# Modulation of a hybrid diffusion backbone: from split weights and vector-engine sums to unsplit float32 matmuls in 32-column tiles

## The chip, the cores and the metric

The kernel runs on one core of one Trainium2 chip. The metric is the device time of one execution in microseconds, as a median over several runs. The engines are PE (matmuls; its weight loads are listed apart as PEld), DVE (vector), ACT (scalar activations), POOL (GpSimd) and SP, which here only issues transfers. Each engine runs its own instructions in a fixed order; semaphores hold an instruction back until what it reads is there.

## The reference, cut to what matters

One layer over 256 latent and 256 context tokens of width 1024. A condition vector `c` (and `c_ctx` for the context) gives six rows of 1024 numbers through `w_ada`, a matrix of 1024 x 6144:

```python
mod = silu(cond) @ w_ada + b_ada
sh1, sc1, g1, sh2, sc2, g2 = split(mod, 6)
pl = split_cols((rms_norm(x) * (1 + sc1) + sh1) @ w_in)     # the context likewise, with c_ctx
x  = x + g1 * (concat(mlstm(pl, pc), hgrn2(pl, pc)) @ w_out)
h  = rms_norm(x) * (1 + sc2) + sh2
x  = x + g2 * moe(h)                                        # top 4 of 32 experts
return rms_norm(x) * final_g
```

`sh1` and `sc1` are wanted at the start, for the latent and for the context; `g1`, `sc2`, `sh2` after the two mixers, and `g2` by the experts, for the latent alone. The mixers are two-directional scans (mLSTM and HGRN2, four heads each), preceded by 3x3 depthwise convolutions. Everything is float32. The 32 experts read 400 MB of weights.

## The kernel before

Tokens stand in 512 columns: 0 to 255 are context, 256 to 511 latent. All large weights come by `load_rows` (L115): a transfer of 1 MB on SP's queue into the next of five buffers of 128 x 2048 (`ring`; for the experts eight and two more). A load can be issued when the buffer five loads earlier has been read out. A projection reads its weight in two halves: `halves` (L86 to L88) makes `wh`, the rounded part (ACT, L87), and `wl`, the rest (DVE, L88), 1024 columns at a time into a pool of three, and three fp32r products, `hh` x `wh`, `hl` x `wh` and `hh` x `wl`, take the place of one in float32 (`proj_cols`, L273 to L275; `proj_tok`, L290 to L292).

A scheduler lays out each engine's order when the kernel is built, from the dependencies, the order of writing and priorities; on the chip the order is fixed, and an instruction that waits holds up all that stand behind it on its engine.

The modulation is done in three ways. Columns 0 to 2047 (`sh1`, `sc1`) go through `halves` like any weight, sixteen of them: the condition (two columns and their rounding rests, `silr`) is the stationary side with 4 columns, and 64 products 4x512 (L239, L240) sum into four banks; `arow`, sixteen small products with `fold4` (L248), `mod` and `gain` follow. The other columns are summed on DVE: `gemv(i, ...)` (L586) runs over eight slices of 128 x 1024 and adds each, times its entry of the condition, to `aacc`; then `row` (L625) sums over the partitions and spreads the row by two float32 products with a matrix of ones, and ACT copies it out (L626). Rows 2 and 4 are summed in `hgrn_inputs(0)`, row 3 after `hgrn_scan(0)`, row 5 (`g2`) late, with its products after the output projection `project(1)`. The sixteen gate columns of `w_in` (`wg`, a transfer of 64-byte pieces) are split into `wgh`, `wgl` (L226, L227) and multiplied in 24 products (L352 to L354).

After the modulation the written order is: projections and scan of the first HGRN2 head pair (`hgrn_inputs(0)`, `hgrn_scan(0)`), of the second pair, the mLSTM inputs and scan (L695 to L741), the output gates (`out_gate`, by `proj_tok`), the output projection, norm and router, and then the experts (L900 to L990). In a scan, L481 is the product on the diagonal, L502 the product of a doubling step, L505 the masked copy behind it, and L531 and L532 update `WW` for the next step.

Of the kernel before, what the change touches and what calls it, by code (L numbers as in the profile page):

```python
# [9 lines left out]
FT = mybir.dt.float32  # L10
FR = mybir.dt.float32r
# [4 lines left out]
OP = mybir.AluOpType  # L16
# [12 lines left out]
def tile_hybrid_backbone(  # L29
# [96 lines left out]
    aacc = [fo.tile([128, D], FT, name=f"aacc{i}") for i in range(3)]  # L126
# [60 lines left out]
    dve.tensor_mul(silc, silc, ptr[:, 0:16])  # L187
    silr = fc.tile([128, 8, 4], FR, name="silr")
    silv = silc.rearrange("p (w k) -> p k w", w=2)
    dve.tensor_copy(silr[:, :, 0:2], silv)  # L190
    dve.tensor_sub(silr[:, :, 2:4], silv, silr[:, :, 0:2].bitcast(FT))
    fold4 = fc.tile([4, 2], FT, name="fold4")
    dve.tensor_add(fold4, ident[0:4, 0:2], ident[0:4, 2:4])
# [25 lines left out]
    wgh = px.tile([128, 8, 128], FR, name="wgh")  # L219
    wgl = px.tile([128, 8, 128], FR, name="wgl")  # L220
    nc.gpsimd.memset(wgh.bitcast(FT), 0.0)
    nc.gpsimd.memset(wgl.bitcast(FT), 0.0)
    wg4 = wg.rearrange("p a (g h) -> p a g h", g=4)
    wgh4 = wgh.rearrange("p a (g r) -> p a g r", g=4)[:, :, :, 0:4]
    wgl4 = wgl.rearrange("p a (g r) -> p a g r", g=4)[:, :, :, 0:4]
    dve.tensor_copy(wgh4, wg4)  # L226
    dve.tensor_sub(wgl4, wg4, wgh4.bitcast(FT))  # L227


    pa = [pj.tile([128, 512], FT, name="pj") for _ in range(4)]  # L230
    for g in range(2):
        for q in range(4):
            w = wa.pop(0) if wa else load_rows(w_ada[0], 256 * q, 2, g * D, D)
            for i in range(2):
                k = 2 * q + i
                wh, wl = halves(w[:, i])
                for n in range(2):
                    s = slice(n * 512, (n + 1) * 512)
                    mm(pa[2 * g + n][0:4, :], silr[:, k], wh[:, s], start=(k == 0), stop=False)  # L239
                    mm(pa[2 * g + n][0:4, :], silr[:, k], wl[:, s], start=False, stop=(k == 7))  # L240

    arow = px.tile([4, 2048], FT, name="arow")
    for n in range(4):
        (act(arow[:, n * 512:(n + 1) * 512], pa[n][0:4, :], AF.Copy) if n % 2 else
         dve.tensor_copy(arow[:, n * 512:(n + 1) * 512], pa[n][0:4, :]))
    pt = bank()
    for b in range(16):
        mm(pt[:, 2 * b:2 * b + 2], arow[:, b * 128:(b + 1) * 128], fold4, start=True, stop=True)  # L248
    mod = fc.tile([128, 16, 2], FT, name="mod")
    dve.tensor_tensor(mod, pt[:, 0:32].rearrange("p (b w) -> p b w", w=2),  # L250
                      cols[:, col["ba"]:col["ba"] + 16].unsqueeze(2).to_broadcast([128, 16, 2]), op=OP.add)
# [179 lines left out]
    def hgrn_inputs(hp, parts=None):  # L431
# [27 lines left out]
    def hgrn_scan(hp, fgt, hq, hv):  # L459
# [114 lines left out]
        return last  # L574

    def gemv(i, dst, after, qs=range(4)):

        if qs[0] == 0:
            nc.gpsimd.memset(dst, 0.0)
            nc.gpsimd.dma_start(dst[0:1, :], b_ada[0:1, i * D:(i + 1) * D])  # L580
        for q in qs:
# [37 lines left out]
    g1b, sc2, sh2 = aacc[0:3]

    def row(i, dst):
        for n in range(2):
            f = slice(n * 512, (n + 1) * 512)
            p_ = bank(True)
            mm(p_, ones, aacc[i][:, f], start=True, stop=True)  # L625
            act(dst[:, f], p_, AF.Identity, bias=one_c) if i == 1 else act(dst[:, f], p_, AF.Copy)  # L626
# [13 lines left out]
    aacc.append(ep.tile([128, D], FT, name="aacc3"))  # L640
# [3 lines left out]
    dve.tensor_mul(sc2, sc2, n2b)  # L644
# [3 lines left out]
    for k in range(8):  # L648
        nc.gpsimd.dma_start(shc[:, k:k + 1], sh2[0:1, k * 128:(k + 1) * 128])
# [185 lines left out]
    gemv(5, aacc[3], scan_end)  # L835
# [23 lines left out]
    nc.gpsimd.dma_start(x2, x[0].rearrange("(a p) d -> p a d", p=128))  # L859
    nc.gpsimd.dma_start(bgs, b_gu[0].rearrange("e (b f) -> (e b) f", f=128).rearrange("(g p) f -> p g f", p=128))  # L860
# [9 lines left out]
    with tc.issue_after(last_e[0].ins):  # L870
        row(3, g2b)
# [237 lines left out]
```

## Time and profile before

| what | value |
|---|---|
| median of 3 runs | 1292.71 us (1290.19 to 1296.00) |
| profiled execution, its own time | 1289.07 us |
| its span | 1287.1 us |
| mean granted TensorE clock | 0.986 of full |
| PE, DVE, ACT, POOL busy | 1165.2, 479.4, 267.9, 110.8 us |
| bytes moved | 455.77 MB |

The span is the time from the first to the last instruction of the profiled execution; some 2 us lie outside it. Busy shares are means over stages with different limits, so the table by stretch (below) says more than they do. Matmuls are pipelined: a product's duration in a row is longer than its distance to the next, and where a price is wanted the distance between starts is the one to take.

### The profile page before, as it was taken

The page shows a single profiled execution, that of the slowest core. Times are in us where ns is not written, and L with a number is a line of the kernel's source. Part 1 is how long each engine was busy: PE and PEld are TensorE (multiplying, and loading weights), DVE is VectorE, ACT ScalarE, POOL GpSimd, SP SyncE. Part 2 cuts the span into 40 slices and gives each one's busy share as a digit, 9 for nine tenths or more (in the row PEclk, how much of TensorE's full clock was granted, in tenths as well). Part 3 has the DMA queues.
Part 4 walks back from the last instruction along what each step waited for, and adds up shares of the span by engine and source line. Part 5 has one row for each costly group of instructions (what it writes and reads, how often), then busy time and mean ns, then how long its engine had stood idle before and what let it go on. Part 6 is the DMA issues. An engine that isn't in the chain of part 4 may idle for free.

```text
span 1287.1 us, 14502 instructions
## 1 busy us (share of the span) xinstructions
PE 1165.2 (91%) x5706; PEld 557.3 (43%) x5709; DVE 479.4 (37%) x983; ACT 267.9 (21%) x492; POOL 110.8 (9%) x199
## 2 busy tenths in 40 slices
PE   4899999998999998889999998998899889889994
PEld 1578998896534342333323422422243234223221
DVE  7889999687112221312112221121211121112124
ACT  5666566563100000001000100100010001000001
POOL 5000000301111010101101100110020002000001
PEclk8899999999999999999999999999999999999998
DMA  9583533349699999999999999999999999999994
GB/s 331 199 294 129 180 102 128 116 173 411 271 416 418 415 418 416 405 417 416 416 416 416 417 417 417 417 417 417 416 417 417 418 417 415 417 417 417 417 415 178
DMA packets 99738, 455.77 MB, mean 354 GB/s; under 512 B 8809, under 2 KB 25282, under 8 KB 66896
## 3 DMA queue, kind: packets, MB, share of 16 engines
q1 hardware_dynamic: 97104, 452.62, 87.7%
q0 software_dynamic: 1200, 1.56, 0.4%
q8 instruction: 47, 0.77, 0.2%
q10 hardware_dynamic: 1360, 0.60, 0.2%
q14 instruction: 27, 0.22, 0.0%
HBM read 453.69 MB, written 1.05 MB: 353 GB/s over the span
## 4 chain that ended last, share of the span: by engine, by line
PE 55%; DMA 37%; DVE 4%; ACT 2%; issue 1%; ACTq 0%; DVEq 0%; SPq 0%
PE pu L940 19%; DMA w<-w_gu_dram 19%; DMA w<-w_down_dram 17%; PE pd L973 9%; PE pm L922 5%; PE pm L985 3%; PE pj L275 2%; PE pj L273 2%; PE pj L274 2%; DVE wl L88 1%; PE pj L292 1%; PE pt L949 1%; DMA wg<-w_in_dram 1%; PE pj L290 1%; PE pj L291 1%
## 5 line engine op out<-in xcount | busy, mean ns | idle before, releaser
L940 PE MATMUL pu<-w,XT 128*64 128x512 f32 x2048 | 470.3, 599 | 31.9 <-DMA w<-w_gu_dram 31.9
L940 PEld LDWEIGHTS pu<-w,XT 128*64 128x64 f32 x2048 | 135.6, 136 | 324.1 <-issue 223.5
L973 PE MATMUL pd<-w,aT 128*64 128x512 f32 x1024 | 240.8, 601 | 16.5 <-DMA w<-w_down_dram 14.9
L956 DVE TENSOR_TENSOR gl<-pt,bgT 128x512 f32<-128x512 f32 x32 | 22.1, 692 | 319.0 <-PE pt L949 318.9
L76 ACT ACTIVATE gu<-pu 128x512 f32<-128x512 f32 x48 | 26.9, 595 | 504.8 <-PE pu L940 504.8
L973 PEld LDWEIGHTS pd<-w,aT 128*64 128x64 f32 x1024 | 65.1, 136 | 152.1 <-issue 101.4
L78 DVE COPY gu<-pu 128x512 f32<-128x512 f32 x16 | 11.1, 692 | 276.4 <-ACT gu L76 276.4
L976 DVE TENSOR_TENSOR YP<-pd,g2b 64x512 f32<-64x512 f32 x64 | 44.1, 689 | 116.8 <-PE pd L973 116.2
L922 PEld LDWEIGHTS pm<-S,h 128*128 128x128 f32 x512 | 65.5, 199 | 47.7 <-issue 44.4
L913 POOL TENSOR_SCALAR S<-islot,posm 128x64 f32<-128x64 f32 x60 | 25.5, 446 | 690.4 <-PE pm L928 660.0
L922 PE MATMUL pm<-S,h 128*128 128x128 f32 x512 | 75.8, 294 | 1.2 <-DVE S L913 1.0
L985 PE MATMUL pm<-YP,GT 128*128 128x512 f32 x128 | 62.6, 615 | 11.0 <-DVE YP L976 11.0
L88 DVE TENSOR_TENSOR wl<-w,wh 128x1024 fp32r<-128x1024 f32 x55 | 66.7, 1221 | 6.5 <-ACT wh L87 6.3
L87 ACT ACTIVATE wh<-w 128x1024 fp32r<-128x1024 f32 x55 | 57.6, 1062 | 44.9 <-PE pj L274 21.8
L924 ACT ACTIVATE XT<-pm 128x512 f32<-128x512 f32 x32 | 19.1, 597 | 224.4 <-PE pm L922 224.4
L275 PE MATMUL pj<-hh,wl 128*128 128x512 f32 (+1 forms) x160 | 58.1, 368 | 3.0 <-DVE wl L88 3.0
L274 PE MATMUL pj<-hl,wh 128*128 128x512 f32 (+1 forms) x160 | 59.0, 370 | 0.0
L273 PE MATMUL pj<-hh,wh 128*128 128x512 f32 (+1 forms) x160 | 58.6, 372 | 0.0
L949 PE MATMUL pt<-ident,gu 128*128 128x128 f32 x256 | 38.8, 282 | 15.2 <-ACT gu L76 15.2
L949 PEld LDWEIGHTS pt<-ident,gu 128*128 128x128 f32 x256 | 27.3, 141 | 53.1 <-ACT gu L76 32.8
L959 ACT ACTIVATE sg<-gl 128x512 f32<-128x512 f32 x32 | 20.2, 630 | 128.5 <-DVE gl L957 128.5
L916 POOL TENSOR_SCALAR G<-islot,posm,gate 128x64 f32<-128x64 f32 x64 | 44.4, 709 | 5.5 <-DVE cnt_i L893 5.0
(455 smaller groups left out, 1210.1 us busy)
## 6 DMA issues: line engine op xcount, KB each, us to landing
w<-w_gu_dram SPq DMA_DIRECT2D x256, 1024.0 KB, 19.9
w<-w_down_dram SPq DMA_DIRECT2D x128, 1024.0 KB, 20.1
w<-w_ada_dram SPq DMA_DIRECT2D x24, 1024.0 KB, 6.4
w<-w_in_dram SPq DMA_DIRECT2D x16, 1024.0 KB, 6.0
w<-w_out_dram SPq DMA_DIRECT2D x4, 1024.0 KB, 5.0
xin<-x_dram SPq DMA_DIRECT2D x1, 1024.0 KB, 7.3
xin<-ctx_dram SPq DMA_DIRECT2D x1, 1024.0 KB, 12.2
x<-x_dram POOLq DMA_DIRECT2D x1, 1024.0 KB, 5.4
```

Of the source, the lines that this page charges most:

```text
L87: act(wh, src, AF.Copy)
L88: dve.tensor_sub(wl, src, wh.bitcast(FT))
L273: mm(o, wh[:, s], hh[:, k, t0:], start=(k == 0), stop=False)
L274: mm(o, wh[:, s], hl[:, k, t0:], start=False, stop=False)
L275: mm(o, wl[:, s], hh[:, k, t0:], start=False, stop=(k == 7))
L916: nc.gpsimd.tensor_scalar(G[:, a, j], islot, pos_of(a, j), gate_of(a, j), op0=OP.is_equal, op1=OP.mult)
L922: mm(p_[:, i * ns:(i + 1) * ns], h2[:, a, (k + i) * 128:(k + i + 1) * 128], S[:, a, 0:nj].rearrange("p j s -> p (j s)"), start=(a == 0), s ...
L940: mm(ps[64 * j:64 * j + 64, n * 512:(n + 1) * 512], XT(k), w[:, 0, j * 1024 + n * 512:j * 1024 + (n + 1) * 512], start=(k == 0), stop=(k = ...
L949: nc.tensor.transpose(pt[:, f * 128:(f + 1) * 128], s[:, f * 128:(f + 1) * 128], ident)
L973: mm(pd_[64 * n:64 * n + 64, :], aT[:, k], w[:, i, n * 512:(n + 1) * 512], start=(k == 0), stop=(k == 7))
L976: dve.tensor_mul(yp[:, f], pd_[64 * n:64 * n + 64, :], g2b[64 * n:64 * n + 64, f])
L985: mm(p_, GTs[j][0:ns, a * 128:(a + 1) * 128], YP[0:ns, j, n * 512:(n + 1) * 512], start=(j == 0), stop=(j == np_ - 1))
```

## The change

The six rows now come from three calls of `gemv(gp)`, 2048 columns each. A call loads eight slices of 128 rows x 2048 columns (one contiguous piece of 8 KB on each partition, where before it was two of 4 KB). For each slice four unsplit float32 products, 128 x 32 on 128 x 512, go to four blocks of 32 partitions of one bank; the 32 stationary columns hold the two conditions and 30 zeros. Call 0 feeds `mod` and `gain` through one copy and four transposes. Calls 1 and 2 are in `rows`, written behind `hgrn_inputs(0)` and behind `hgrn_inputs(1)`: DVE adds the bias, POOL sends the row to DRAM and reads it back spread over the partitions; `g2b` is read back later. `shc`, once eight small transfers, comes from four transposes. The sums on DVE, the products with ones and sixteen of the splits are gone. The modulated tokens are now written in place in `hT`; the gate columns are unsplit too, in eight float32 products with 32 columns, and one product with `sel4` adds their four blocks.

```diff
-    wa = [load_rows(w_ada[0], 0, 2, 0, D)]
     nc.sync.dma_start(xin[:, 2:4], x[0].rearrange("(a p) d -> p a d", p=128))
-    wa.append(load_rows(w_ada[0], 256, 2, 0, D))
     nc.sync.dma_start(xin[:, 0:2], cx[0].rearrange("(a p) d -> p a d", p=128))
...
-    dve.tensor_copy(wgh4, wg4)
-    dve.tensor_sub(wgl4, wg4, wgh4.bitcast(FT))
...
+    dve.tensor_copy(wgp[:, :, 0:16], wg)
...
+    def gemv(gp):
+
+        pa = pj.tile([128, 512], FT, name="pj")
+        for k in range(8):
+            w = load_rows(w_ada[0], 128 * k, 1, 2 * D * gp, 2 * D)
+            for j in range(4):
+                mm(pa[32 * j:32 * j + 32, :], silr[:, k], w[:, 0, j * 512:(j + 1) * 512], start=(k == 0), stop=(k == 7))
+        return pa
+
+    def columns(p_, row):
+
+        for i in range(4):
+            nc.tensor.transpose(p_[:, i * 128:(i + 1) * 128], row[:, i * 128:(i + 1) * 128], ident)
+        return p_.rearrange("p (c j r) -> p j c r", c=4, j=4)
+
+    pa = gemv(0)
+    arow = px.tile([128, 512], FT, name="arow")
+    act(arow, pa, AF.Copy)
...
+        hm = hT[:, k]
+        act(hm[:, 0:256], hm[:, 0:256], AF.Identity, bias=mod[:, k, 1:2], scale=gain[:, k, 1:2])
+        dve.tensor_scalar(hm[:, 256:], hm[:, 256:], gain[:, k, 0:1], mod[:, k, 0:1], op0=OP.mult, op1=OP.add)
         act(hh[:, k], hm, AF.Copy)
...
+    pg4 = pj.tile([128, 512], FT, name="pj")
+    for k in range(8):
+        mm(pg4[32 * (k % 4):32 * (k % 4) + 32, :], wgp[:, k], hT[:, k], start=(k < 4), stop=(k >= 4))
+    gq = px.tile([128, 512], FT, name="gq")
+    act(gq, pg4, AF.Copy)
     pg = pj.tile([128, 512], FT, name="pj")
-    for k in range(8):
-        mm(pg, wgh[:, k], hh[:, k], start=(k == 0), stop=False)
-        mm(pg, wgh[:, k], hl[:, k], start=False, stop=False)
-        mm(pg, wgl[:, k], hh[:, k], start=False, stop=(k == 7))
+    mm(pg, sel4, gq, start=True, stop=True)
...
-            w = load_rows(w_ada[0], 256 * q, 2, i * D, D)
-            for j in range(2):
-                k = 2 * q + j
-                with tc.issue_after(after.ins):
-                    dve.scalar_tensor_tensor(dst, w[:, j], silc[:, k:k + 1], dst, op0=OP.mult, op1=OP.add)
+    def rows(gp):
+
+        t = ar[gp - 1]
+        dve.tensor_add(t, t, gemv(gp))
+        nc.gpsimd.dma_start(scr[gp - 1].rearrange("(j f) -> j f", f=512), t[0:128:32, :])
+        for i, o in enumerate((g1b, sh2) if gp == 1 else (sc2,)):
+            nc.gpsimd.dma_start(o, bcast(scr[gp - 1, i * D:(i + 1) * D], D))
...
     h0 = hgrn_inputs(0, first)
-    scan_end = hgrn_scan(0, *h0)
+    rows(1)
+    hgrn_scan(0, *h0)
     h1 = hgrn_inputs(1)
...
-    gemv(3, aacc[2], scan_end)
-    for i in range(3):
-        row(i, aacc[i])
+    rows(2)
     mlstm_v()
-    scan_end = hgrn_scan(1, *h1)
+    hgrn_scan(1, *h1)
     mlstm_qk()
...
-    for k in range(8):
-        nc.gpsimd.dma_start(shc[:, k:k + 1], sh2[0:1, k * 128:(k + 1) * 128])
+    dve.tensor_copy(shc.rearrange("p (j c) -> p j c", j=2), columns(bank(True), ar[0])[:, 2:4, :, 0])
...
-    gemv(5, aacc[3], scan_end)
...
+    nc.gpsimd.dma_start(g2b, bcast(scr[1, D:2 * D], D))
...
-    with tc.issue_after(last_e[0].ins):
-        row(3, g2b)
```

Line numbers of the changed kernel are some lines lower for what is unchanged: a projection's products L273 to L275 are L272 to L274 there, L481 and L502 are L479 and L500, L505 is L503.

DVE at the start, around the gate columns, in the kernel before (`rs` and `r` are the inverse root of a row norm, two tokens' tiles at a time, `xin` the scaled tokens):

```order
L103 TENSOR_TENSOR rs_163<-rs_163,rs_162 128x2
L226 CAST wgh<-wg 128x32x4
L104 SCALAR_TENSOR_TENSOR r_157<-rs_163,r_157 128x2
L227 TENSOR_TENSOR wgl<-wg,wgh 128x32x4
L102 TENSOR_TENSOR rs_163<-r_157 128x2
L88 TENSOR_TENSOR wl<-w,wh 128x1024
```

The same place in the changed kernel:

```order
L204 TENSOR_SCALAR xin<-xin,r_159 128x1024
L95 TENSOR_SCALAR rs_185<-rs_183 128x2
L96 TENSOR_SCALAR rs_184<-rs_183 128x2
L221 COPY wgp<-wg 128x8x16
L97 TENSOR_SCALAR r_159<-rs_185 128x2
L102 TENSOR_TENSOR rs_185<-r_159 128x2
```

The instruction that waits for `wg` stands in the first norm (latent) before and in the second norm (context) now; both times norm work of the tokens is behind it.

PE from the sums of the modulation to the first projection, before:

```order
L240 MATMUL pj<-wl,silr 4x512 x2
L248 MATMUL m<-fold_154,arow 128x2 x8
L352 MATMUL pj<-hh,wgh 128x512
L273 MATMUL pj<-hh,wh 128x512 x3
L353 MATMUL pj<-hl,wgh 128x512
L354 MATMUL pj<-hh,wgl 128x512
```

And in the changed kernel:

```order
L235 MATMUL pj<-w,silr 32x512 x12
L241 MATMUL m<-ident,arow 128x128 x4
L351 MATMUL pj<-hT,wgp 32x512 x8
L355 MATMUL pj<-gq,sel_259 128x512
L272 MATMUL pj<-hh,wh 128x512
L273 MATMUL pj<-hl,wh 128x512
```

Before, gate products and the first projection took turns as `hh` came slice by slice; now all gate products, and the one that reads ACT's copy `gq` of them, stand ahead of the first projection.

PE at the first scan, before (two pieces of one long run of projection products, which belong to the second head pair):

```order
L275 MATMUL pj<-hh,wl 128x512
L481 MATMUL m<-hq,kl 128x128 x4
L273 MATMUL pj<-hh,wh 128x512
L274 MATMUL pj<-hl,wh 128x512
L275 MATMUL pj<-hh,wl 128x512
L273 MATMUL pj<-hh,wh 128x512
```

```order
L502 MATMUL m<-ql,kl 128x128 x4
L273 MATMUL pj<-hh,wh 128x512
L274 MATMUL pj<-hl,wh 128x512
L275 MATMUL pj<-hh,wl 128x512
L273 MATMUL pj<-hh,wh 128x512
```

And in the changed kernel, behind the last product of the first pair's value projection:

```order
L274 MATMUL pj<-hh,wl 128x512
L235 MATMUL pj<-w,silr 32x512 x20
L479 MATMUL m<-hq,kl 128x128 x4
L500 MATMUL m<-ql,kl 128x128 x4
L235 MATMUL pj<-w,silr 32x512 x4
L500 MATMUL m<-ql,kl 128x128 x4
L235 MATMUL pj<-w,silr 32x512 x4
L500 MATMUL m<-ql,kl 128x128 x4
L235 MATMUL pj<-w,silr 32x512 x4
L500 MATMUL m<-ql,kl 128x128 x4
L272 MATMUL pj<-hh,wh 128x512
```

The scan's first products stood among projection products before; now the 32 products of `gemv(1)` and four steps of the scan stand between one projection and the next, and four products further on the transposes of the second value convolution (L453) and a fifth step. The second scan has the same picture, with `gemv(2)` and the output gates' products behind it.

## Rows read from the trace of the kernel before

**Rows 1.** Busy time by stretch: stretch, us, PE, PEld, DVE, ACT, POOL, PEclk, DMA share, GB/s.
```profile
0.00:51.70 51.70, 27.64 (x131) 13.61 (x133) 43.05 (x95) 32.24 (x43) 16.54 (x41) 0.92 0.91 324
51.70:227.20 175.50, 172.43 (x1025) 149.95 (x1025) 162.29 (x307) 106.44 (x167) 5.10 (x12) 0.98 0.47 155
227.20:281.50 54.30, 54.05 (x360) 46.25 (x362) 42.28 (x121) 34.50 (x103) 9.28 (x14) 1.00 0.45 161
281.50:324.00 42.50, 35.29 (x185) 28.07 (x183) 32.77 (x123) 18.61 (x41) 5.95 (x5) 0.92 0.78 321
324.00:340.00 16.00, 16.00 (x84) 9.03 (x86) 0.15 (x1) 1.47 (x3) 6.04 (x12) 0.90 0.45 177
340.00:1287.00 947.00, 859.82 (x3928) 310.36 (x3924) 198.82 (x340) 74.69 (x137) 67.92 (x116) 0.99 1.00 408
```

**Rows 2.** The chain of waits that ends last, from 0 to 420: start us, us, what.
```profile
1.74 16.43 DMA wg<-w_in_dram
18.19 0.86 DVE wgh L226
...
301.88 1.72 PE pj L772 x4
...
310.89 0.50 ACT g2b L626
311.43 1.12 PE t L625 x2
...
323.97 5.29 PE pm L922 x32
329.48 7.02 PE pu L940 x32
```

**Rows 3.** DMA queues from 6 to 16 us: packets, MB, share of 16 engines.
```profile
q1 hardware_dynamic: 961, 3.74, 94.7%
q10 hardware_dynamic: 943, 0.06, 6.6%
```

**Rows 4.** Groups by shape, 0 to 324 us: busy us, mean ns | idle before, releaser.
```profile
L88 DVE TENSOR_TENSOR wl<-w,wh 128x1024 fp32r<-128x1024 f32 x55 | 66.7, 1221 | 6.5 <-ACT wh L87 6.3
L87 ACT ACTIVATE wh<-w 128x1024 fp32r<-128x1024 f32 x55 | 57.6, 1062 | 44.9 <-PE pj L274 21.8 <-PE pj L239 5.8 <-PE pj L292 5.6
...
L586 DVE SCALAR_TENSOR_TENSOR aacc<-w,silc,aacc 128x1024 f32<-128x1024 f32 x32 | 40.7, 1281 | 0.1
...
L310 DVE SCALAR_TENSOR_TENSOR ac<-pre,cols,ac 128x189 f32<-128x189 f32 x48 | 19.2, 412 | 0.1
...
L310 DVE SCALAR_TENSOR_TENSOR ac<-pre,cols,ac 128x252 f32<-128x252 f32 x24 | 11.3, 476 | 0.0
...
L505 DVE COPY_PREDICATED hsT<-lmask,m 128x256 f32<-128x256 uint8 x28 | 10.9, 447 | 0.0
...
L531 DVE TENSOR_TENSOR WW<-WW,tn 128x512 f32<-128x512 f32 x12 | 8.3, 691 | 0.1
...
L325 ACT ACTIVATE hh<-hm 128x512 fp32r<-128x512 f32 x8 | 4.5, 615 | 0.0
...
L316 DVE SCALAR_TENSOR_TENSOR hq<-ac,pre 128x256 f32<-128x256 f32 x4 | 1.6, 421 | 1.5 <-ACT pre L314 1.5
```

**Rows 5.** The chain of waits, 95 to 125 us, at the first scan.
```profile
115.35 0.24 PE pj L274
115.81 0.89 PE m L481 x8
116.94 0.24 PE pj L274
```

**Rows 6.** PE in order of time: start us, us, instruction (two neighbours of 256 columns).
```profile
151.53 0.28 PE L292 MATMUL pj<-wh,hl 128*128 128x256 f32 x1
151.65 0.28 PE L290 MATMUL pj<-wh,hh 128*128 128x256 f32 x1
```

**Rows 7.** The page's costliest groups: the weight loads beside L940.
```profile
L940 PEld LDWEIGHTS pu<-w,XT 128*64 128x64 f32 x2048 | 135.6, 136 | 324.1 <-issue 223.5
```

More of the change, by code (lines that the diff above doesn't have):

```diff
@@ L125, in tile_hybrid_backbone @@
     fo = front.enter_context(tc.tile_pool(name="fo", bufs=1))
-    aacc = [fo.tile([128, D], FT, name=f"aacc{i}") for i in range(3)]
+    g1b, sc2, sh2 = [fo.tile([128, D], FT, name=f"row{i}") for i in range(3)]
+    ar = [fo.tile([128, 512], FT, name=f"ar{i}") for i in range(2)]
+    dr = ctx.enter_context(tc.tile_pool(name="dr", bufs=1, space=bass.MemoryType.DRAM))
+    scr = dr.tile([2, 2 * D], FT, name="scr")
     hss = fo.tile([128, 2, 8], FT, name="hss")
@@ L180, in tile_hybrid_backbone @@
         nc.gpsimd.dma_start(gb[32 * g:32 * g + 4, :], ml_gate_b[0, g].rearrange("(h o) -> h o", o=1))
+    for i in range(2):
+        nc.gpsimd.memset(ar[i], 0.0)
+        nc.gpsimd.dma_start(ar[i][0:128:32, :], b_ada[0, 2 * D * (i + 1):2 * D * (i + 2)].rearrange("(j f) -> j f", f=512))
     ptr = bank()
@@ L186, in tile_hybrid_backbone @@
     act(silc, ptr[:, 0:16], AF.Sigmoid)
[L187 to L193, printed above, removed]
+    silr = fc.tile([128, 8, 32], FT, name="silr")
+    nc.gpsimd.memset(silr, 0.0)
+    dve.tensor_mul(silr[:, :, 0:2], silc.rearrange("p (w k) -> p k w", w=2), ptr[:, 0:16].rearrange("p (w k) -> p k w", w=2))
     ss = fc.tile([128, 4], FT, name="ss")
@@ L216, in tile_hybrid_backbone @@
     hc0 = 128 + col["hc"]
[L219 to L225, printed above, removed]
-    dve.tensor_copy(wgh4, wg4)
-    dve.tensor_sub(wgl4, wg4, wgh4.bitcast(FT))
-    pa = [pj.tile([128, 512], FT, name="pj") for _ in range(4)]
@@ L231, in tile_hybrid_backbone @@
[L231 to L248, printed above, removed]
+    wgp = px.tile([128, 8, 32], FT, name="wgp")
+    nc.gpsimd.memset(wgp, 0.0)
+    dve.tensor_copy(wgp[:, :, 0:16], wg)
+    sel16 = px.tile([128, 16], FT, name="sel16")
@@ new lines, in tile_hybrid_backbone @@
+    dve.tensor_reduce(sel16, ident.rearrange("p (j r) -> p r j", r=32)[:, 0:16], axis=AX.X, op=OP.add)
+    sel4 = px.tile([128, 128], FT, name="sel4")
+    nc.gpsimd.memset(sel4, 0.0)
+    dve.tensor_copy(sel4.rearrange("p (g r) -> p g r", g=4)[:, :, 0:4], sel16.rearrange("p (g h) -> p g h", g=4))
+    def gemv(gp):
[5 more added lines that the diff above has]
+        return pa
@@ L249, in tile_hybrid_backbone @@
+    def columns(p_, row):
[5 more added lines that the diff above has]
+    act(arow, pa, AF.Copy)
     mod = fc.tile([128, 16, 2], FT, name="mod")
-    dve.tensor_tensor(mod, pt[:, 0:32].rearrange("p (b w) -> p b w", w=2),
-                      cols[:, col["ba"]:col["ba"] + 16].unsqueeze(2).to_broadcast([128, 16, 2]), op=OP.add)
+    dve.tensor_tensor(mod.rearrange("p (j c) w -> p j c w", j=4), columns(bank(), arow)[:, :, :, 0:2],
+                      cols[:, col["ba"]:col["ba"] + 16].rearrange("p (j c) -> p j c", j=4).unsqueeze(3).to_broadcast([128, 4, 4, 2]),
+                      op=OP.add)
@@ L321, in tile_hybrid_backbone @@
     for k in range(8):
-        hm = px.tile([128, 512], FT, name="hm", bufs=2)
-        act(hm[:, 0:256], hT[:, k, 0:256], AF.Identity, bias=mod[:, k, 1:2], scale=gain[:, k, 1:2])
-        dve.tensor_scalar(hm[:, 256:], hT[:, k, 256:], gain[:, k, 0:1], mod[:, k, 0:1], op0=OP.mult, op1=OP.add)
+        hm = hT[:, k]
+        act(hm[:, 0:256], hm[:, 0:256], AF.Identity, bias=mod[:, k, 1:2], scale=gain[:, k, 1:2])
+        dve.tensor_scalar(hm[:, 256:], hm[:, 256:], gain[:, k, 0:1], mod[:, k, 0:1], op0=OP.mult, op1=OP.add)
         act(hh[:, k], hm, AF.Copy)
-        last_hl = dve.tensor_sub(hl[:, k], hm, hh[:, k].bitcast(FT))
+        dve.tensor_sub(hl[:, k], hm, hh[:, k].bitcast(FT))
     lbw = fc.tile([128, 4], FT, name="lbw")
@@ L558, in hgrn_scan @@
             o = 1 if d_ == 0 else 0
-            last = dve.tensor_mul(kc[:, d_], kc[:, d_], sc[:, :, o:o + 256])
+            dve.tensor_mul(kc[:, d_], kc[:, d_], sc[:, :, o:o + 256])
         for h in range(2):
@@ L573, in hgrn_scan @@
             act(yh[:, a, 256 * hp:256 + 256 * hp], po[:, 0:256], AF.Copy)
[L574 to L581, printed above, removed]
-            w = load_rows(w_ada[0], 256 * q, 2, i * D, D)
-            for j in range(2):
-                k = 2 * q + j
-                with tc.issue_after(after.ins):
-                    dve.scalar_tensor_tensor(dst, w[:, j], silc[:, k:k + 1], dst, op0=OP.mult, op1=OP.add)
+    def rows(gp):
[4 more added lines that the diff above has]
+            nc.gpsimd.dma_start(o, bcast(scr[gp - 1, i * D:(i + 1) * D], D))
     def mlstm_qk():
@@ L615, in tile_hybrid_backbone @@
     h0 = hgrn_inputs(0, first)
-    scan_end = hgrn_scan(0, *h0)
+    rows(1)
+    hgrn_scan(0, *h0)
     h1 = hgrn_inputs(1)
[L619 to L626, printed above, removed]
-    gemv(3, aacc[2], scan_end)
-    for i in range(3):
-        row(i, aacc[i])
+    rows(2)
     mlstm_v()
-    scan_end = hgrn_scan(1, *h1)
+    hgrn_scan(1, *h1)
     mlstm_qk()
@@ L643, in tile_hybrid_backbone @@
     nc.sync.dma_start(n2b, bcast(norm2_g, D))
-    dve.tensor_mul(sc2, sc2, n2b)
+    dve.scalar_tensor_tensor(sc2, sc2, 1.0, n2b, op0=OP.add, op1=OP.mult)
     rw = ep.tile([128, 8, NE], FT, name="rw")
```

4 lines of the change are left out of this document (removed).

## Prediction

> **What bounds the kernel now.** I read the table by stretch first [rows 1]. From 340 us to the end the DMA share is 1.00 at 408 GB/s: the experts' weights set the pace there, and their bytes do not change. Between 324 and 340 the share is 0.45: all expert buffers are full, and the first can only come free when the first expert has been multiplied. So the end moves one for one with the moment at which the experts begin (L922 at 323.97, L940 at 329.48 [rows 2]), and the question is what happens in the 324 us ahead. The largest stretch there, 51.7 to 227.2, is PE's: busy 172.4 of 175.5 us, against 162.3 of DVE and a DMA share of 0.47 [rows 1]. What is taken from DVE there gains nothing by itself; what is added to PE's in-order row, or makes PE wait, is paid. The stretch before 51.7 is a chain of loads, splits and norms; 227 to 324 alternates between PE and DVE.
>
> The profiled execution took 1289.07 us, 3.6 below the median of 1292.71 and 1.1 below the lowest of the three runs (1290.19 to 1296.0). I add to 1289.07.
>
> **The front, up to the end of the first two projections.** Gone are 16 splits (16 x 1.22 of DVE, 16 x 1.06 of ACT [rows 4]) and 64 products. But something else is late. In 6 to 16 us the bulk queue moved 961 packets and the gate columns' queue 943 [rows 3]: each DMA engine takes them in turn, one bulk packet of 4 KB and one of 64 bytes, about 60 pairs an engine in 10 us, 0.167 a pair. `wg` is 64 small packets an engine, and it lands at 18.2, where DVE was waiting for it (L226 [rows 2]). The loads of `w_ada` now have 8 KB pieces, so a pair should take twice as long, 0.33. With some 12 pairs beside the tokens' 4 KB pieces from 6 us on and 52 beside 8 KB ones, `wg` lands near 6 + 2.0 + 17.3 = 25.3. The copy of it (L221) stands on DVE ahead of the context's norm, so the tokens are scaled near 29, their transposes follow on PE ahead of the third group of `gemv(0)`, and the eighth load, which needs the third buffer back, can be issued only near 33.7 and lands near 38.5. The last four products, `arow`, four transposes, `mod` and `gain` end near 45.6. Then ACT's row is 3 splits of 1.06, 8 modulations and 8 roundings (0.615 each by L325, nearer 0.55 apart, as neighbours overlap [rows 4]) and `gq`, about 12.1 us, and since `gq` is read by the product that stands ahead of the first projection, that begins near 57.7 instead of 51.7: **+6.0**. Off PE behind it go the 24 gate products, which are projection products of 512 columns at 0.234 (0.24 where the row is rounded [rows 5]), **-5.6**. That is even, +0.4. If `wg` lands as before, the front is some 7.5 shorter.
>
> **The two other calls of gemv.** On PE's row in the stretch that PE bounds. One load is four side-by-side products of 512 columns. L940 puts two blocks side by side: 32 of its records start within 7.02 us [rows 2], 0.439 for a pair of records, and one 512-column product of 128 x 128 is two records in 0.86 (L772, x4 in 1.72 [rows 2]). So a pair of blocks costs what one product costs, 0.877 for both, and I take that four blocks cost the same: 8 x 0.877 = 7.0 a call, **+14.0** for two. The bound on the other side is four products one after another, 3.44 a load, 27.5 a call. I take the low end since the two blocks of L940 overlap wholly. The products with ones go: three of the four rows stood in this stretch, 6 x 0.86, **-5.2**.
>
> The Trainium skill ("TensorE: Matmul & The Clock Gate", section The mechanism) says that a weight load overlaps matmuls in flight only when its row group differs; the four blocks here use all rows, so by that rule the eight weight loads of a group would stand in line. L940's are 136 ns each [rows 7] and its blocks share their rows too, yet a record follows the last in 0.219 us, so the trace disagrees with the rule for two blocks. By the rule a call would be 8 x (0.877 + 8 x 0.136) = 15.7, an estimate. It is rival E below. The same page of the Trainium skill (section Measured speedup vs the span model) has three column blocks at 2.38 times, which would make a call some 9 us, an estimate; no run here shows four.
>
> **What the new order does to PE.** In the kernel before, the scan's first product stands between products of the next projections (L274 at 115.35, L481 at 115.81, L274 at 116.94 [rows 5]): while DVE works off convolutions and doubling steps, PE never waits. In the changed order all 32 products of `gemv(1)` and the first five steps of the scan stand ahead of the bulk of these projections. What DVE must do from the end of the query projection until the value transposes and the fifth step are ready, counted in its new order: 36 taps (16 at 0.412, 8 at 0.476, 8 of 192 at 0.41, 4 of 255 at 0.48: 15.6), three closing products of the convolutions (2 x 0.42 and 0.69), two query products 1.4, four updates of 256 at 0.42 and six of 512 at 0.69 (5.8), two scans and two products of the gates 2.7, six masked copies 2.7, the bias 0.7: 30.4 us, all at the prices of [rows 4] or of the row nearest in width. To this come ACT's turns between (copies, sigmoid, the two operands of a step), about four at once on the chain, by L316's wait and width some 4.5 us. That is 35. PE's own row in that time: 48 products of the value projection at 0.234 (11.2), one call (7.0), six scan products of 0.89 [rows 5], the transposes 0.9 and four products 0.9: 25.4. PE would wait 9.6 us, and the second scan, with `gemv(2)`, is laid out alike: **+19**. The bounds are 0 (DVE is ahead of its row when the scan begins, or a turn is hidden) and 28 (each of the turns costs 1 us more).
>
> **Work moved ahead.** 69 products of the output gates, at 0.12 [rows 6], stand ahead of the mLSTM scan now and stood behind its start: **+8.2**, given back later, **-8.2**. At the beginning of the mLSTM scan DVE's key convolution has 21 us of DVE work ahead of PE's first product by the new order, some 4 us more than PE has; PE was idle 3.1 of the 175.5 us before [rows 1]: **+1.0**. Behind the output projection `row(3)` is gone from the chain, from 310.89 to 312.56: ACT's 0.5, the products' 1.12 [rows 2] and the turn between, with the first product ahead of it: **-2.2**. Of the splits on the chain behind 281 (1.22 each [rows 4]) one lies earlier in the new order, **-1.2**.
>
> The detour through DRAM I cost at nothing: its transfers are issued on POOL near 130 and 200 us and read after 290, with a DMA share of 0.47 between; POOL is busy 5.1 us of that stretch [rows 1]. If the cover were gone, 2 MB at 408 GB/s is 5 us. The in-place modulation adds no wait that the two orders show.
>
> **Sum.** +0.4 + 14.0 - 5.2 + 19 + (8.2 + 1.0) - (8.2 + 2.2 + 1.2) = +25.8: 1289.07 + 25.8 = **1315**. PE's work ahead of the experts hardly changes; PE's waits do.
>
> **Rivals.**
> A, the forecast: 1315, with its own range of 1303 to 1330 from the bounds above.
> B, the scan does not park PE. DVE loses 32 x 1.281 us of sums and 16 splits [rows 4]; if it is ahead of PE by that when the first scan begins, the nineteen vanish: 1296. For it: DVE's load. Against it: the convolutions cannot begin before their projection ends, so being ahead does not help them. Within 0.5%.
> C, faster. `wg` lands near 18 as before (the 8 KB pieces go out as two packets), the first projection starts near 50, the scan does not park PE, and in 227 to 324, where PE is busy for 89 of 97 us [rows 1], the lighter DVE gives back 5 of the 8: 1315 - 19 - 10 - 5 = 1281. It decides by whether a product of the next projection follows the value projection within some 15 us.
> D, the four blocks do not run side by side; 3.44 a load. The waits of PE at the scans are then filled by the longer calls, 27.5 - 7.0 - 9.6 = +11 each, and the first call adds some 8 at the front: 1345. L940 speaks against it, for two blocks; four are not in the trace.
> E, the four blocks overlap, but each weight load of 0.136 [rows 7] stands in line: 8 x 8 x 0.136 = 8.7 more a call. At the scans that lies inside the wait of 9.6; in the front half of it, paced by loads, is seen: 1319. L940's 0.219 a record speaks against it. It is the Trainium skill's rule named above.
>
> **How the numbers follow.** A 0.54, B 0.17, C 0.10, D 0.08, E 0.04; 0.07 for what I do not see, both ways. A measurement of this kernel tells about 0.5%, 6.5 us, from no change, by runs that span 5.8. Slower by more: A, D, E, some of B and of the rest, 0.72. Within: most of B and some of the rest, 0.17. Faster: C and a little, 0.11. The range leaves out D and half of C and reaches over A's and B's bounds: 1282 to 1330.
>
> **What would show it.** Right: the copy of `wg` on DVE waits for its transfer until 24 to 26 us; the first projection starts at 56 to 59; `gemv(1)` and `gemv(2)` take 0.9 a load; PE idles some 10 us behind each value projection, with the fourth or fifth step of the scan behind DVE; the mLSTM scan starts 35 to 42 us later than 227, the experts 22 to 30 later than 324. Wrong: no idle PE at the scans (B); records of L235 over 0.4 us apart (D; 0.25 to 0.4, E); `wg` at 18 and experts before 318 (C); or the experts' stretch itself longer than 947 us [rows 1], which nothing in the change explains.

## The result, and the profile after

| | before | changed |
|---|---|---|
| median | 1292.28 us (1290.19 to 1296.00) | 1307.32 us (1306.54 to 1309.57) |
| span of the profiled execution | 1287.1 us | 1304.8 us |
| mean granted clock | 0.986 | 0.979 |
| DVE busy, ACT busy | 479.4, 267.9 us | 422.5, 246.5 us |
| experts begin (L922, now L900) | 323.97 us | 340.57 us |

The changed kernel is slower: 1.0125 times, interval 1.0103 to 1.0148, or +15.0 us. DVE lost 57 us of work and ACT 21, and the time is longer all the same. Behind the first dispatch of the experts nothing changed (963.1 us before, 964.2 now, to the end of the span), so the loss lies in the 324 us ahead, where the prediction looked for it.

Busy time by stretch of the changed kernel, columns as in [rows 1]. The stretches are cut at the first product of the first projection (55.08), at the first product of the third, the query projection (80.57), and at the first product of the mLSTM scan (256.7):

```profile
0.00:55.08 55.08, 22.70 (x121) 9.65 (x123) 27.49 (x88) 23.24 (x39) 13.90 (x40) 0.81 0.83 308
55.08:80.57 25.49, 25.49 (x107) 19.44 (x106) 14.34 (x30) 16.92 (x21) 0.21 (x2) 0.95 0.23 78
80.57:256.70 176.13, 166.26 (x1098) 139.22 (x1096) 125.08 (x283) 85.56 (x150) 11.51 (x18) 0.98 0.53 183
256.70:340.60 83.90, 76.00 (x459) 63.64 (x458) 56.81 (x194) 44.53 (x118) 8.09 (x8) 0.94 0.53 207
```

The same marks in the kernel before:

```profile
0.00:52.28 52.28, 28.20 (x132) 14.10 (x134) 43.63 (x96) 32.64 (x43) 16.54 (x41) 0.92 0.91 323
52.28:82.49 30.21, 30.21 (x120) 23.90 (x118) 24.92 (x31) 20.14 (x29) 0.00 (x0) 0.91 0.56 192
82.49:227.20 144.71, 141.66 (x906) 125.56 (x905) 136.79 (x277) 85.91 (x138) 5.10 (x12) 1.00 0.45 148
227.20:324.00 96.80, 89.34 (x543) 74.33 (x544) 75.06 (x242) 53.11 (x143) 15.23 (x19) 0.96 0.59 231
```

The two tables account for the whole difference. Up to the third projection the change gains 1.9 us (80.57 against 82.49). Behind it, up to the experts, PE was busy 231.0 and idle 10.5 us before; it is busy 242.3 and idle 17.8 now: -1.9 + 11.3 + 7.3 = +16.7, and the experts begin 16.6 later. PE idles more and works longer, on about the same products.

The start. DVE in order of time: the copy of the gate columns and what ended its wait.

```profile
25.38 0.23 DVE L221 COPY wgp<-wg 128x128 f32<-128x128 f32 x1 [12.06 <-DMA wg<-w_in_dram]
```

The DMA queues from 6 to 16 us, columns as in [rows 3]:

```profile
q1 hardware_dynamic: 636, 3.99, 96.1%
q10 hardware_dynamic: 604, 0.04, 4.2%
```

Again one small packet goes with one bulk packet, but only 604 of the 1024 small ones in these 10 us, where it was 943 [rows 3]. From the chain of waits (start us, us, what), the way into the first projection and into the experts:

```profile
54.06 2.01 PE pj L355 x2
56.07 0.43 PE pj L272
...
340.57 5.56 PE pm L900 x32
346.34 7.02 PE pu L918 x32
```

The one product that adds the gates' four blocks took 2.01 us, and the first products of the projection follow at 0.43 us instead of 0.23: PE had been idle 3.6 us ahead of them, and the granted clock is 0.57 of full in 54 to 58. The kernel before is no better off there: its granted clock is 0.91 over the first two projections, against 0.95 now.

The first scan on PE, in order of time (start us, us, instruction, idle before it and what ended it):

```profile
97.53 4.50 PE L235 MATMUL pj<-w,silr 128*32 128x512 f32 x40
101.96 1.16 PE L479 MATMUL m<-hq,kl 128*128 128x128 f32 x8
102.96 1.06 PE L500 MATMUL m<-ql,kl 128*128 128x128 f32 x8
103.95 1.06 PE L235 MATMUL pj<-w,silr 128*32 128x512 f32 x8
104.94 1.16 PE L500 MATMUL m<-ql,kl 128*128 128x128 f32 x8
106.11 1.07 PE L235 MATMUL pj<-w,silr 128*32 128x512 f32 x8
108.30 1.16 PE L500 MATMUL m<-ql,kl 128*128 128x128 f32 x8 [1.12 <-ACT ql L493]
109.39 1.07 PE L235 MATMUL pj<-w,silr 128*32 128x512 f32 x8
111.81 1.16 PE L500 MATMUL m<-ql,kl 128*128 128x128 f32 x8 [1.36 <-ACT ql L493]
113.28 0.50 PE L272 MATMUL pj<-hh,wh 128*128 128x512 f32 x1 [0.31 <-ACT wh L87]
```

Eight records are four products, the work on one slice of 128 rows. Such a group of four blocks costs 0.99 us between steps of the scan (103.95 to 104.94) and 0.89 in a row (five groups from 97.53 to 101.96). ACT's `ql`, behind DVE's update, ends the waits of the steps, and DVE is busy for all of the 14 us from 100 to 114. These waits, with 0.54 at the fifth step, are 3.3 us; in the second scan the same list gives 4.2.

### The profile page after: what moved, and what is told of

Same layout as the page of the kernel before. It is cut to its first block, busy times and chain, and to the rows that moved or that the text cites. A ratio compares the mean times of both kernels' runs of the same rounds, so it can differ in the third digit from the quotient of the medians.

```text
span 1304.8 us, 14569 instructions
## 1 busy us (share of the span) xinstructions
PE 1166.1 (89%) x5790; PEld 551.6 (42%) x5791; DVE 422.5 (32%) x934; ACT 246.5 (19%) x467; POOL 106.1 (8%) x194
## 4 chain that ended last, share of the span: by engine, by line
PE 53%; DMA 35%; DVE 5%; ACT 2%; issue 1%; ACTq 0%; DVEq 0%; SPq 0%
PE pu L918 18%; DMA w<-w_gu_dram 18%; DMA w<-w_down_dram 17%; PE pd L951 8%; PE pm L900 5%; PE pm L963 3%; PE pj L274 2%; PE pj L273 2%; PE pj L272 2%; PE pt L927 1%; PE pj L291 1%; PE pj L290 1%; PE pj L289 1%; DVE ac L309 1%; PE m L709 1%; PE m L569 1%
## 5 line engine op out<-in xcount | busy, mean ns | idle before, releaser
L900 PEld LDWEIGHTS pm<-S,h 128*128 128x128 f32 x512 | 65.7, 200 | 48.4 <-issue 45.2
L900 PE MATMUL pm<-S,h 128*128 128x128 f32 x512 | 76.1, 295 | 1.2 <-DVE S L891 1.0
L272 PE MATMUL pj<-hh,wh 128*128 128x512 f32 (+1 forms) x160 | 59.7, 373 | 0.3 <-ACT wh L87 0.3
L902 ACT ACTIVATE XT<-pm 128x512 f32<-128x512 f32 x32 | 19.1, 597 | 215.8 <-PE pm L900 215.8
L88 DVE TENSOR_TENSOR wl<-w,wh 128x1024 fp32r<-128x1024 f32 x39 | 47.3, 1222 | 37.7 <-ACT wh L87 37.5
L274 PE MATMUL pj<-hh,wl 128*128 128x512 f32 (+1 forms) x160 | 58.3, 366 | 0.0
L273 PE MATMUL pj<-hl,wh 128*128 128x512 f32 (+1 forms) x160 | 58.3, 365 | 0.0
L87 ACT ACTIVATE wh<-w 128x1024 fp32r<-128x1024 f32 x39 | 41.0, 1069 | 19.7 <-PE pj L291 11.4
```

The source lines that it names most:

```text
L87: act(wh, src, AF.Copy)
L88: dve.tensor_sub(wl, src, wh.bitcast(FT))
L272: mm(o, wh[:, s], hh[:, k, t0:], start=(k == 0), stop=False)
L273: mm(o, wh[:, s], hl[:, k, t0:], start=False, stop=False)
L274: mm(o, wl[:, s], hh[:, k, t0:], start=False, stop=(k == 7))
L900: mm(p_[:, i * ns:(i + 1) * ns], h2[:, a, (k + i) * 128:(k + i + 1) * 128], S[:, a, 0:nj].rearrange("p j s -> p (j s)"), start=(a == 0), s ...
```

## The experiments

**The front alone, and the rows alone.** Of the two parts of the change, one at a time. The first keeps the new start and puts the sums on DVE and the products with ones back:

```diff
-    rows(1)
-    hgrn_scan(0, *h0)
+    scan_end = hgrn_scan(0, *h0)
     h1 = hgrn_inputs(1)
-    rows(2)
+    gemv(3, aacc[2], scan_end)
+    for i in range(3):
+        row(i, aacc[i])
```

> One part of the change alone: sh1 and sc1, the gates and the modulation in place as in the changed kernel (eight loads of 2048 columns, 32-column tiles), but the other four rows summed on DVE and spread by products with ones as in the kernel before. Theory (the front is about even: the second projection's last product started at 80.3 in the changed kernel against 82.2 before; the loss lies in the rows): 1288 to 1293. Rival (the late first projection, 55 against 51.7, is what costs): 1297 or more.

The second keeps the old start and its gates:

```diff
-    gemv(3, aacc[2], scan_end)
-    for i in range(3):
-        row(i, aacc[i])
+    rows(2)
```

(and `rows(1)` behind `hgrn_inputs(0)`.)

> The other part alone: front and gates as in the kernel before (splits, 4-column products), and g1, sc2, sh2, g2 by the 32-column products, DRAM and the two calls of rows at their places in the changed kernel. Theory (the loss lies in these products and in their place): 1306 to 1311, PE waiting 3 to 5 us in each of the two scans. Rival (the front makes the loss): 1292 to 1297.

The front alone took 1280.77 us, ratio 0.9918 (0.9899 to 0.9937); the rows alone 1312.11, ratio 1.0152 (1.0132 to 1.0172). The change is a gain of 11 and a loss of 20 in one diff. I had expected the front to be even and missed its size; the rows alone came out 1 us above what I expected. The last two stretches of the front alone, cut at the same marks:

```profile
79.42:220.40 140.98, 140.98 (x907) 125.25 (x905) 131.65 (x263) 84.54 (x138) 4.16 (x11) 1.00 0.44 144
220.40:313.20 92.80, 84.58 (x540) 71.20 (x541) 74.77 (x243) 52.02 (x143) 17.00 (x22) 0.97 0.63 238
```

The third projection begins 3.1 us earlier than before, and the 233.8 us behind it are 7.7 shorter: PE idles 8.2 instead of 10.5 us and is busy 225.6 instead of 231.0. Between the third projection and the mLSTM scan it has no idle time here. Before, it waited there twice for DVE's `wl`, 3.0 us in all, and this is the longer of the two:

```profile
85.96 0.51 PE L275 MATMUL pj<-hh,wl 128*128 128x256 f32 x2 [2.73 <-DVE wl L88]
```

Of the 5.4 us of busy time the clock (0.97 of 92.8 against 0.96 of 96.8 us) explains about 1. Another 2.8 are the first products of the mLSTM scan, `mk` on `mq` with 64 rows: thirty-two records, which took 9.3 us before and take 6.5 now. Four records between projection products before, and eight in a row in the front alone:

```profile
231.74 1.13 PE L695 MATMUL m<-mq,mk 64*128 64x256 f32 x4
```

```profile
227.52 1.14 PE L691 MATMUL m<-mq,mk 64*128 64x256 f32 x8
```

So the order is worth something here too. No run tests why eight go in the time of four, and the rest of the 5.4 us is open. In the rows alone the same two marks are these:

```profile
82.35:262.00 179.65, 168.73 (x1104) 140.87 (x1102) 129.49 (x295) 88.69 (x154) 11.75 (x20) 0.97 0.53 184
262.00:346.50 84.50, 76.36 (x459) 64.01 (x460) 56.76 (x194) 44.33 (x118) 8.02 (x7) 0.94 0.53 206
```

19.1 us idle and 245.1 busy: the picture of the changed kernel, from a start that is the old one. The wait for `wl` is gone here as well, and the mLSTM products take 6.8 us, as they do in the changed kernel.

**The place of the rows.** The same products, written later:

```diff
-    rows(1)
     hgrn_scan(0, *h0)
     h1 = hgrn_inputs(1)
-    rows(2)
     mlstm_v()
     hgrn_scan(1, *h1)
     mlstm_qk()
+    rows(1)
+    rows(2)
```

> The changed kernel with rows(1) and rows(2) written behind mlstm_qk() instead of behind hgrn_inputs(0) and hgrn_inputs(1); the front is the same, the same 64 products of L235 remain. In its order the first scan stands among the next pair's projection products again, and the 64 products stand at the end of the second scan and the start of the mLSTM scan. Theory (the place of the products costs: PE waited 3.3 and 4.2 us in the two scans and then ran at half clock for some 3): these 10 us go, and some of the 15 us of products fill waits of PE before the mLSTM scan: 1292 to 1297. Rival (the products' own PE time is the whole cost, wherever they stand): 1305 to 1308.

1288.37 us, ratio to before 0.9969 (0.9953 to 0.9985): 19 less than the changed kernel, more than I expected. Up to the third projection and from there to the experts:

```profile
0.00:56.05 56.05, 21.96 (x121) 9.38 (x123) 30.56 (x88) 23.25 (x39) 13.92 (x40) 0.80 0.85 302
56.05:82.45 26.40, 26.40 (x107) 20.15 (x106) 14.31 (x30) 17.04 (x21) 0.21 (x2) 0.92 0.22 65
82.45:321.70 239.25, 231.66 (x1554) 195.37 (x1554) 181.66 (x477) 132.53 (x270) 18.57 (x26) 0.99 0.57 209
```

Against the changed kernel PE idles 7.6 instead of 17.8 us and is busy 231.7 instead of 242.3, with the same products: 10.2 + 10.6 - 1.9 (a start that is later by that) = 18.9, the whole difference. Of the 10.6 some 6 are the granted clock, by an estimate from the rounded values: 0.98 of 176 and 0.94 of 84 us are 8.5 us lost, 0.99 of 239 is 2.4. So it is the place of the 64 products, with the order that it brings, that makes the change slower than the kernel before. They are not free when they stand late either: the front alone is 7.6 us faster (1280.77). The rest, about 4, goes with steps that take 0.99 us and more beside products of 32 columns, where eight records of a step took 0.89 [rows 5]; no run separates it.

**The price of the products.** With one slice of eight:

```diff
+                if gp == 0 or k == 0:
-                mm(pa[32 * j:32 * j + 32, :], silr[:, k], w[:, 0, j * 512:(j + 1) * 512], start=(k == 0), stop=(k == 7))
+                    mm(pa[32 * j:32 * j + 32, :], silr[:, k], w[:, 0, j * 512:(j + 1) * 512], start=(k == 0), stop=(k == 7 or gp > 0))
```

> The changed kernel, in which gemv(1) and gemv(2) multiply only the first of their eight slices (g1, sc2, sh2 and g2 are sums over 128 of 1024 rows): 56 of 64 products of 32 columns are gone, all loads stay. With so few products the order leaves both scans among projection products, as with the rows written late. The time against that of the rows written late (1288) is then what 14 groups of four cost where they stand there. Theory (there they fill waits of PE, which was idle 14.7 us in all behind 50 us): 1283 to 1288. Rival (they are paid on PE at 0.93 a group): 1274 to 1277.

The experts begin at 309.57, 12.1 us ahead of the kernel with the rows late. (The whole took 1632.75 us. The rows that go on to the router and the experts hold other numbers here, and the part behind took 1319 us instead of 964; its cause was not looked for, and only the part ahead is read.) Fourteen groups at 0.93 are 13.0, so the rival held and the theory fell: where PE is kept busy the products are paid almost in full, 0.86 a group by this difference of two kernels, whose orders differ too. They fill no waits: PE idles 5.5 us without the fourteen groups and 7.6 with them.

```profile
82.10:309.60 227.50, 221.97 (x1442) 196.26 (x1442) 181.77 (x477) 129.26 (x268) 18.61 (x26) 0.98 0.54 196
```

**The gate columns at the start.** Two ways to take away what the wait at 25.38 costs. The copy on POOL, behind which nothing waits:

```diff
-    dve.tensor_copy(wgp[:, :, 0:16], wg)
+    nc.gpsimd.tensor_copy(wgp[:, :, 0:16], wg)
```

> The changed kernel with one instruction moved: the copy of the sixteen gate columns (L221), which waited on DVE until 25.4 us ahead of the context's norm, goes to POOL; the orders of PE, ACT and SP are the same. Theory (the wait for the 64-byte pieces, stretched by the 8 KB pieces beside them, holds up norm, transposes, the third group of products and so the eighth load): the tokens' transposes start near 16 instead of 28.3 us, the first projection near 46 to 48 instead of 55, and the time falls by 7 to 9, to about 1299. Rival (the loads pace the front anyway): the transposes start early but the first projection stays at 54 to 56 and the time at 1307.

The loads of the first call cut into pieces of 4 KB:

```diff
+        if pieces:
+            for h in range(2):
+                f = slice(c0 + h * 1024, c0 + h * 1024 + 1024)
+                nc.sync.dma_start(t[:, h * 1024:(h + 1) * 1024], w[r0:r0 + 128, f])
+            return v
```

> The changed kernel with the eight loads of gemv(0) alone cut into two transfers each, so that their contiguous pieces are 4 KB as before instead of 8 KB; the copy of the gate columns stays on DVE. Theory (the 64-byte pieces of the gate columns take turns with the bulk pieces on each DMA engine, so they land twice as late beside pieces twice as long): the copy's wait ends near 18 to 19 us as in the kernel before, the first projection starts near 48 to 51, the time falls by 4 to 8, to 1299 to 1303. Rival (they are late for another reason, their place in the queues or the loads' number): the wait still ends at 24 to 26 and the time stays at 1307.

On POOL: 1298.03 us, 9.3 less than the changed kernel (ratio to before 1.0053, 1.0033 to 1.0073); the first projection starts at 46.77 instead of 55.08. With 4 KB pieces: 1303.99, 3.3 less (1.0105, 1.0074 to 1.0136); first projection at 50.26. The wait on DVE and the DMA queues from 6 to 16 us of the latter:

```profile
17.75 0.23 DVE L226 COPY wgp<-wg 128x128 f32<-128x128 f32 x1 [7.41 <-DMA wg<-w_in_dram]
```

```profile
q1 hardware_dynamic: 1006, 3.73, 93.4%
q10 hardware_dynamic: 983, 0.06, 6.7%
```

The pieces' size sets the landing: 17.75 with 4 KB, 25.38 with 8 KB, with nearly the same bytes (3.7 and 4.0 MB) moved in those 10 us. The wait and the first projection came as the theory said; the time is 1 us above its range. That the second edit gains less than the first has a reason in the order: the copy had moved up seven rows on DVE, ahead of the instruction that makes `silr`, so that PE's first group of the call started at 19.0 instead of 12.6.

**Both helps together, and the best of the parts.** The copy on POOL with the rows late, and the copy on POOL with the front alone:

> Both of the edits that helped, together: the copy of the gate columns on POOL (1298.0 alone) and the rows behind the mixers (1288.4 alone), on the changed kernel (1307.3). Theory (two waits in different stretches, both ahead of the experts): the gains add, 9.3 + 18.9: 1277 to 1281. Rival (they are the same slack): 1286 to 1289.

> The front of the changed kernel with the other rows on DVE as before (1280.8) and the copy of the gate columns on POOL. Theory (the wait for the gate columns costs the same 9 us there): 1270 to 1274. Rival (DVE, which has 32 sums more there, takes the gain): 1277 to 1281.

1278.36 us (0.9899, 0.9871 to 0.9926) and 1272.88 (0.9857, 0.9827 to 0.9886). The gains add, within 1.4 us: they lie in different stretches, both ahead of the experts. The second beats both kernels, by 18.5 and 34 us.

**The first projection ahead of the gates.** The remaining wait of the start, in the changed kernel and in the best one:

```diff
+    first = proj_cols(2576, (0, 0), first)
     pg4 = pj.tile([128, 512], FT, name="pj")
```

> The changed kernel with the first projection written ahead of the gate products: most of its 48 products stand on PE ahead of the one product that reads ACT's copy of the gates (L355), which held the first projection back until 55.1 us. Theory (PE was idle or at half clock behind the roundings while it waited for that copy): the first projection starts near 50, at the pace of the roundings, and the time falls by 2 to 5, to 1302 to 1305. Rival (the roundings pace it anyway, the second projection ends where it did): 1306 to 1308.

> The best kernel so far (new front, copy of the gate columns on POOL, other rows on DVE: 1272.9), with the first projection written ahead of the gate products. By the same theory the second projection ends 2 to 5 us earlier and the time is 1268 to 1271; by the rival it stays at 1272 to 1274.

Neither theory held. The changed kernel became slower by 8, 1315.27 (1.0195, 1.0178 to 1.0212), which neither expectation had, though the third projection began 2.3 us earlier (78.25). The best kernel stayed where it was, as the rival said: 1274.24 (0.9876, 0.9860 to 0.9892), though its third projection began 3.0 us earlier (68.65 against 71.69). In the slower one the first scan shows where the time goes, by stretch and then on PE in order of time:

```profile
98.00:106.00 8.00, 6.07 (x52) 2.29 (x50) 5.74 (x15) 7.32 (x12) 0.00 (x0) 0.99 0.67 230
106.00:112.00 6.00, 6.00 (x36) 3.41 (x40) 6.00 (x17) 2.30 (x4) 0.00 (x0) 0.73 1.01 378
112.00:118.00 6.00, 3.40 (x20) 1.78 (x12) 6.00 (x14) 4.88 (x7) 0.08 (x1) 0.84 1.10 349
118.00:124.00 6.00, 5.34 (x16) 4.37 (x17) 6.00 (x12) 2.44 (x4) 1.05 (x3) 0.50 1.08 379
```

```profile
105.98 2.08 PE L501 MATMUL m<-ql,kl 128*128 128x128 f32 x8 [1.93 <-ACT ql L494]
...
118.02 2.07 PE L501 MATMUL m<-ql,kl 128*128 128x128 f32 x8 [0.83 <-ACT ql L494]
```

PE waits 1.93 us at the second step, where the changed kernel had no wait, the clock falls to its lower level twice, and the steps and the projection behind them run at half speed. From the third projection to the second scan the kernel loses 10.2 us, of which 3.1 are more idle time and some 6.8 the granted clock (0.73, 0.84, 0.50 and, from 124 to 130, 0.80). It is 7.9 us late at the second scan and still 7.9 late at the experts.

PE did not come early to that scan. Its first product there starts at 102.90, against 101.96 in the changed kernel, and DVE comes late. The edit put the gate products behind the first projection, and so the chain of the mLSTM gates on ACT and DVE, too, moved back, into the convolutions ahead of the scan. DVE's first instruction of that chain and its operands of the scan's first doubling step, in the changed kernel:

```profile
62.42 0.68 DVE L385 SCALAR_TENSOR_TENSOR hsT<-hsT 36x512 f32<-36x512 f32 x1 [7.07 <-ACT hsT L384]
...
93.91 1.29 DVE L468 TENSOR_TENSOR WW<-hq,fgt 128x512 f32<-128x512 f32 x2
```

And with the first projection ahead of the gates:

```profile
78.71 0.68 DVE L386 SCALAR_TENSOR_TENSOR hsT<-hsT 36x512 f32<-36x512 f32 x1 [4.15 <-ACT hsT L385]
...
102.34 0.43 DVE L315 SCALAR_TENSOR_TENSOR hq<-ac,pre 128x256 f32<-128x256 f32 x1 [2.23 <-ACT pre L313]
102.80 1.29 DVE L469 TENSOR_TENSOR WW<-hq,fgt 128x512 f32<-128x512 f32 x2
```

The chain begins 16.3 us later and the operands come 8.9 later. What PE won ahead of the gates was lost in the scan to work that the same edit pushed there; no run moves the first projection and leaves the chain where it was. In the best kernel the operands are not late (96.95 against 99.29), and the mLSTM scan still begins 2.6 us earlier (210.35 against 212.94), but the experts only 0.4. Behind 285 us the granted clock is 0.87 instead of 0.98 there, which is about 2.4 us, by an estimate from the rounded values.

## Why the prediction was right, by its steps

The direction, its cause by place, and the range held: 1315 was forecast from 1289.07, +25.8; the experts begin 16.6 later and the median is 15.0 higher. One term was too large by more than half, and two were missing. That the sum came so near owes something to luck: the waits at the scans were put 11.5 us too high, and some 4.6 us of clock that the sum does not have, with a wait of 2.2 us ahead of the mLSTM scan where 1.0 was put, fill part of that gap. Of the signs that were named, the wait for `wg` and the price of a load came true; the idle time at the scans, the start of the mLSTM scan and that of the experts (22 to 30 later was said) came out smaller, and the first projection began 0.9 us ahead of its range.

- **The gate columns.** Landing at 25.3 was forecast, 25.38 measured, by the mechanism given (17.75 with pieces half as long). Tokens scaled near 29 (28.9), first projection near 57.7 (55.1). The third projection was to begin 0.4 later and began 1.9 earlier.
- **The price of the calls.** 7.0 a call was forecast, 0.877 a group; it measured 0.89 in a row, 0.99 between scan steps, and 0.86 by the experiment that took fourteen away. Four blocks overlap as two did. Rivals D and E are out: weight loads in line would have made a group 1.96. The rule on row groups in the Trainium skill ("TensorE: Matmul & The Clock Gate", section The mechanism) is not borne out here for four column blocks either.
- **PE parked at the scans: the step that failed in size.** 9.6 us a scan were forecast, 3.3 and 4.2 measured, 7.5 in place of 19. The order was read rightly, and of the nine waits all but two of 0.31 (the splits') are ended by ACT's `ql` or by DVE, as said. From the end of the query projection (86.2) to the fifth step (115.8) it is 29.6 us where 35 was forecast, and PE's own work in it is 26.3 where 25.4 was. The 30.4 us of DVE work in the 35 were wrong: they were summed from mean durations, and neighbours on DVE overlap. In the changed kernel's own order of time:

```profile
98.21 0.42 DVE L309 SCALAR_TENSOR_TENSOR ac<-pre,cols,ac 128x189 f32<-128x189 f32 x1 [0.53 <-ACT ac L299]
98.54 0.48 DVE L311 SCALAR_TENSOR_TENSOR ac<-pre,cols,ac 128x255 f32<-128x255 f32 x1
98.94 0.41 DVE L309 SCALAR_TENSOR_TENSOR ac<-pre,cols,ac 128x192 f32<-128x192 f32 x1
...
105.69 0.69 DVE L529 TENSOR_TENSOR WW<-WW,tn 128x512 f32<-128x512 f32 x1
106.29 0.69 DVE L530 TENSOR_TENSOR WW<-WW,tn 128x512 f32<-128x512 f32 x1
```

  A tap of 0.42 is followed after 0.33, an update of 0.69 after 0.60: some 0.08 too much on each of about 60 instructions is 5 us a scan. The prediction had taken this care for PE (distances between starts) and not for DVE.
- **The clock: missing.** After the waits of the second scan the granted clock is 0.50 in 184 to 187, and a step of eight records took 2.01 us. The clock's share of the loss, 0.98 of 176 and 0.94 of 84 us against 1.00 of 145 and 0.96 of 97 before, is about 4.6 us, an estimate from these rounded values.
- **What is gained behind the front: missing.** Alone, the front gained 11 where +0.4 was forecast. The parts do not add: at the experts' start they give -10.8 and +22.6 alone, which is +11.8, and together they gave +16.6. Two gains stand in both parts and come only once in the whole: the 3.0 us of waiting for `wl`, which is gone in each of them, and some 2.5 us of the mLSTM products (9.3 before, 6.5 and 6.8 in the parts, 6.8 together). That is 5.5 of a difference of 4.8. The forecast had neither.
- **Moved ahead and given back.** The mLSTM scan starts 29.5 later, where 35 to 42 was forecast; 12.9 are given back by the experts' start, where 11.6 was forecast. The detour through DRAM cost nothing, as forecast: in the changed kernel only POOL waits for it, PE, DVE and ACT never, and its three transfers of 512 KB landed 9.6 us after their issue.

Rival B (the scans do not park PE, 1296) and C (and the columns land early, 1281) did not happen. The experiments made something like both: with the rows late PE has no wait in the two scans (1288), and with the copy on POOL besides, no norm waits for the columns (1278). Of the 26.5 us by which the changed kernel is slower than the front alone, 18.9 go with the place of the rows, that is, with an order that the scheduler laid out; 7.6 stay when they stand late.

## What to carry to other kernels

When work moves from an engine with slack to the in-order engine that bounds a stretch, read in the new order what it pushes apart: here 56 products cost 12 us where they stood among other work, and together with the order that they brought 31 where they stood between the steps of a scan. Price a chain by distances between starts on every engine, not by durations. An edit that brings one thing forward pushes another back: look for that one on the other engines before the gain is booked. And look at what small transfers share an engine with: beside bulk pieces of 8 KB a 64 KB load of 64-byte pieces was there at 25.4 us, beside 4 KB at 17.75, and the instruction that waits for it belongs on an engine with nothing behind it.

## What the runs showed of the hardware that was not expected

The granted clock fell to its lower level inside a scan, twice, in the slower kernel of the last experiment: right behind a wait of 1.93 us among short products (0.53 in 106 to 109.5), and, after it had been 1.00 in 110 to 115.5, behind waits of 1.32 and 0.47 us (0.51 in 116 to 126). In the changed kernel the first scan's waits of 1.12 and 1.36 us brought no fall (1.00 in 100 to 114); the second scan's five, 4.2 us together, did (0.50 in 184 to 187). And four products of 32 columns, unsplit float32 and 512 wide, cost 0.89 to 0.99 us by their starts, little more than one product of 128 columns (0.86 [rows 2]). Eight records of products with 64 rows took 1.14 us in a row, where four took 1.13.
